# First squares, level sums and pooling sums from GpSimd to VectorE and ScalarE, and the pooling products one unit later

## The chip, the core and the metric

The kernel runs on one core of a Trainium2 chip. The metric is the device time of one execution in microseconds (us). Engines are named as the profile names them: PE (TensorE, matrix products), DVE (VectorE), ACT (ScalarE), POOL (GpSimd) and SP (SyncE, which here only issues DMAs). Each engine works through its own instructions in the order in which they were written.

## What is computed

Two layers of a decoder, for 256 tokens of a prompt and 8 sequences of 8 new tokens (320 tokens in all), with width 2048 and shared weights, in 32-bit floats:

```python
def trunk(...):
    for l in range(DEPTH):
        h = rmsnorm(x, norm_mix[l])
        m, s, b = mixer(h, ...)            # below
        x = x + m
        h = rmsnorm(x, norm_ffn[l])
        x = x + (jax.nn.silu(h @ w_gate[l]) * (h @ w_up[l])) @ w_down[l]
    return rmsnorm(x, norm_final), ...

def mixer(h, s_gla, buf, ...):
    proj = h @ w_in                        # q, k, v, g, gk_lr, u
    gk = jax.nn.log_sigmoid(gk_lr @ w_gk_up + b_gk) / GK_NORM
    o, s_new = gla(q, k, v, gk, s_gla)     # gated linear attention, causal
    o = rmsnorm(o, gla_norm) * jax.nn.silu(g)
    p, buf_new = pool_mixer(u, buf, ...)
    out = jnp.concatenate([o, p], axis=-1) @ w_out

def pool_mixer(u, buf, ...):               # windows 2, 4, 8, 16 for four groups of channels
    ext = jnp.concatenate([buf, u], axis=1)
    # per group: trailing mean over its window minus the token, then a 256x256 map
    y = einsum(mean - u, w_pool) * pool_scale
```

## The kernel before

Everything is kept transposed: features on the 128 partitions, the 320 tokens along a row. All weights pass through one stream of units. A unit is a block of up to 4 row tiles by 256 columns (512 KB); PE multiplies it into two output tiles of 128 x 320. To keep 32-bit accuracy each operand is split into a high and a low part, and every product is done three times (`mm3`, L145 to L147: high by high, high by low, low by high): 24 matmuls for a unit, 12 for a unit of a pooling map (two row tiles).

The loop `run` goes through the units. For unit i it loads up to unit i + 5 (four buffers `raw`, DMAs on SP), splits up to unit i + 2 (three buffers `hl`: ACT casts the high part at L109, DVE subtracts the low part at L110), reads out the accumulators that the unit before completed ("due" functions, `ev_...`), issues the unit's matmuls, and then lets every running generator do one step. The order in which the program text does this is the order of each engine's instructions; no scheduler moves anything. There are four accumulator tiles `acc`, two for a pair of output tiles.

The units of a layer's mixer stand in the order `IN_ORDER`: k and q, then u (the pooling inputs, four pairs 3, 2, 1, 0), then v and g. The pooling map of a group is a unit of its own (`pool_units`, "product 3" to "product 0" below), put among the four units of a later pair: product 3 among those of u1, product 2 among those of u0, and products 1 and 0 among those of v0.

Three pieces of work that the change touches run beside the stream:

- `first_squares` (L907 to L932 of before): the sum over features of x squared for the first norm, in tiles `qah` and `qal`, while the first weights and x arrive. `make_r` sums it over partitions with a matmul into `ps_r`, from which `r`, the norm's factor, is made.
- `level_gen`: the attention scores by eight levels of halving. Each level adds neighbouring sums in place: L430 on the half `Xv` (tile `PX`), L432 on the half `Pv` of the same tile, 640 elements a partition at levels 1, 2, 4 and 512 at the other five.
- `ev_u` and `pool_gen`: the outputs of a u pair are written into `EP` (prompt) and `ES` (samples) by DVE, the head of `ES` by a copy from `stg`, which SP loads. Trailing sums are then doubled, `AP` over `EP` (L578) and `AS` over `ES` (L579): one, two, three or four steps for windows 2, 4, 8, 16. L585 mends the first 16 positions, `so` takes the rows that go out by DMA (L592), and `d`, split into `dh` and `dl`, is the operand of the product. The product's outputs are read out by `split2` into `ph` (ACT, L122) and `pl` (DVE, L127).

Of the kernel before, what the change touches and what calls it, by code (L numbers as in the profile page):

```python
# [35 lines left out]
# columns of `vecs`, one 128-row column per feature tile  # L36
# [5 lines left out]
# pairs of 128-column tiles of w_in, in the order in which they are multiplied  # L42
# [12 lines left out]
class Unit:  # L55
    """A block of weights: nk row tiles by 256 columns, used by two output tiles."""
# [7 lines left out]
class Decoder:  # L64
# [40 lines left out]
    def split(self, hi, lo, src, scale=None):  # L105
        """hi + lo = src * scale, each of them with the 12 bits that the array multiplies."""
        nc = self.nc
        if scale is None:
            nc.scalar.copy(hi, src)  # L109
            nc.vector.tensor_tensor(lo, src, hi.bitcast(F32), ALU.subtract)  # L110
        else:
            nc.scalar.activation(hi, src, AF.Copy, scale=scale)  # L112
            nc.vector.scalar_tensor_tensor(lo, src, scale, hi.bitcast(F32), ALU.mult, ALU.subtract)  # L113

    def split2(self, his, los, srcs, scales=(None, None)):
        """Two splits, so that neither engine waits for the other's half."""
        nc = self.nc
        for hi, x, s in zip(his, srcs, scales):
            if s is None:
                nc.scalar.copy(hi, x)  # L120
            else:
                nc.scalar.activation(hi, x, AF.Copy, scale=s)  # L122
        for hi, lo, x, s in zip(his, los, srcs, scales):
            if s is None:
                nc.vector.tensor_tensor(lo, x, hi.bitcast(F32), ALU.subtract)
            else:
                nc.vector.scalar_tensor_tensor(lo, x, s, hi.bitcast(F32), ALU.mult, ALU.subtract)  # L127

    def rsqrt(self, out, src, scale):
        """out = 1 / sqrt(src * scale + EPS): exp(-log / 2), then a Newton step."""  # L130
        nc = self.nc
        h, t, y = (self.nrm.tile([P, T], F32, tag="rs_" + n, name="rs_" + n) for n in "hty")
        nc.scalar.activation(t, src, AF.Ln, scale=scale, bias=self.eps)
        nc.scalar.activation(y, t, AF.Exp, scale=-0.5)
        nc.vector.tensor_scalar(h, src, -0.5 * scale, -0.5 * EPS, ALU.mult, ALU.add)
        nc.vector.tensor_tensor(t, y, y, ALU.mult)
        nc.vector.tensor_tensor(t, t, h, ALU.mult)
        nc.vector.scalar_tensor_tensor(out, t, 1.5, y, ALU.add, ALU.mult)

# [9 lines left out]
    def pair_units(self, srcs, order, rhs, evac, nk=4):  # L149
        """Units that make one pair of output tiles: srcs[i] holds row tiles 4 i .. 4 i + 3."""  # L150
        box = {}
        units = []
        for n, i in enumerate(order):
            def mm(hl, n=n, i=i):
                if n == 0:
                    box["ps"] = [self.acc.tile([P, 512], F32, tag="acc", name="acc") for _ in range(2)]
                for j in range(2):
                    for k in range(nk):
                        xh, xl = rhs(i * nk + k)
                        self.mm3(box["ps"][j][:, :T], hl, k, j, xh, xl,  # L160
                                 n == 0 and k == 0, n == len(order) - 1 and k == nk - 1)
            ev = (lambda: evac([t[:, :T] for t in box["ps"]])) if n == len(order) - 1 else None
            units.append(Unit(srcs[i], nk, mm, ev))
        return units
# [52 lines left out]
    def add_square(self, m, x):  # L217
        """Adds x * x into the running sum over feature tiles."""
# [9 lines left out]
    def make_r(self):  # L228
        """After the last square: r = rsqrt(mean + eps) on every partition."""
        yield  # L230
        ps = self.smt("ps_r")
        self.nc.tensor.matmul(ps[:, :T], self.ones, self.sq_acc, start=True, stop=True)
        self.r = self.nrm.tile([P, T], F32, tag="r", name="r", bufs=2)
        yield
        self.rsqrt(self.r, ps[:, :T], 1.0 / D_MODEL)

    def new_x(self, ms, l, base):
        """Two tiles of x are final: the operands with the next norm's weight, and the squares."""
# [13 lines left out]
    def mixer_units(self, l):  # L252
# [7 lines left out]
        for n, (kind, i) in enumerate(IN_ORDER):  # L260
# [3 lines left out]
            if (kind, i) == ("v", 0):  # L264
                us[3:3] = self.pool_units(l, 0)
                us[2:2] = self.pool_units(l, 1)
            if (kind, i) == ("v", 1):
                us[0].start = self.open_late
            if kind == "u" and i < 2:
                us[2:2] = self.pool_units(l, i + 2)  # L270
# [4 lines left out]
        # w_out: the pooling half of the rows first  # L275
# [51 lines left out]
    def gk_gen(self, l):  # L327
        """log of the gates: P = 16 * gk = log_sigmoid(z), z = h w_gk w_gk_up + b."""
# [6 lines left out]
        # [hi | lo] of a row tile side by side: one pass multiplies both  # L335
# [31 lines left out]
    def level_gen(self):  # L367
        """Scores k_j . q_i exp(b_i - b_j) for j <= i, transposed. Tokens are halved again and
        again: at level s, a pair with i in the second and j in the first half of a group of 2 s
        takes exp(sum from the half's start to i) on q and exp(sum from j to the half's end) on k,  # L370
        so that no exponent is above zero."""
# [31 lines left out]
        for li, s in enumerate((1, 2, 4, 8, 16, 32, 64, 128)):  # L403
# [26 lines left out]
            nc.gpsimd.tensor_tensor(Xv[:, :, :, 0, :], Xv[:, :, :, 0, :],  # L430
# [3 lines left out]
            if s == 4:  # L434
                # whole sequences of the sample group
# [45 lines left out]
        # k decayed to the end of the prompt  # L481
# [23 lines left out]
    def put(self, p0, w, c0, src, copy=None):  # L505
        """Scores of both prompt tiles and all heads into rows p0.., columns c0.. of a tile."""
        # tile 0 starts at column 0 of a head's 384, tile 1 at 256
# [4 lines left out]
    def kd_sample(self):  # L512
        """k decayed to the end of its sequence, as 32 rows a sequence: hi, lo, hi, lo."""
# [22 lines left out]
    def stack(self, x, out, his, los):  # L536
        """x [P, n, 8, 8] into out [P, n, 8, 4, 8] as rows hi (at his) and lo (at los)."""
# [10 lines left out]
    # -- pooling  # L548
    def ev_u(self, ps, i):
# [12 lines left out]
        nc.gpsimd.tensor_copy(ES[:, :, :, 0:BUF], stg)  # L562
        self.gens.append(self.pool_gen(l, i, EP, ES))

    def pool_gen(self, l, i, EP, ES):
# [4 lines left out]
        # sums over trailing windows, doubling; only what the last one needs  # L570
# [3 lines left out]
        while s < w:  # L574
# [3 lines left out]
            nc.gpsimd.tensor_tensor(ap[:, :, lo:], cp[:, :, lo:], cp[:, :, lo - s : np_ - s], ALU.add)  # L578
            nc.gpsimd.tensor_tensor(as_[:, :, lo:], cs[:, :, lo:], cs[:, :, lo - s : ns_ - s], ALU.add)  # L579
# [4 lines left out]
        # the sequence's start: fewer positions than the window  # L584
        nc.gpsimd.tensor_tensor(cp[:, :, BUF : BUF + 16], cp[:, :, BUF : BUF + 16],  # L585
                                self.wcnt[:, i : i + 1, :].to_broadcast([P, 2, 16]), ALU.mult)
        # the buffers that go on: the last 15 rows
        so = early.tile([P, 2, NB + 1, BUF], F32, tag="so", name="so")
        nc.gpsimd.tensor_copy(so[:, :, 0:NB, :], ES[:, :, :, NS:])
        nc.gpsimd.tensor_copy(so[:, :, NB, :], EP[:, :, NP:])  # L590
# [32 lines left out]
    # -- values and gates, one head at a time  # L623
# [7 lines left out]
    def head_gen(self, h, vT):  # L631
# [33 lines left out]
        # rows of one sequence at a time, zero elsewhere  # L665
# [192 lines left out]
    def build(self):  # L858
# [4 lines left out]
        # x and the first weights arrive in turn  # L863
# [8 lines left out]
        # the array's clock rises once it has been busy for a while  # L872
# [34 lines left out]
    def first_squares(self):  # L907
        nc = self.nc
        q = [self.ffb.tile([P, 8, T], F32, tag=t, name="q" + t) for t in ("ah", "al")]
        for c in range(2):  # L910
            x = self.xT[:, 4 * c : 4 * c + 4, :]
            nc.gpsimd.tensor_tensor(q[0][:, 4 * c : 4 * c + 4, :], x, x, ALU.mult)
        add = lambda a, b: nc.gpsimd.tensor_tensor(a, a, b, ALU.add)
        add(q[0][:, 0:4], q[0][:, 4:8])
        for c in range(2):
            for _ in range(2):
                yield
            v = q[1][:, 4 * c : 4 * c + 4]
            nc.scalar.activation(v, self.xT[:, 8 + 4 * c : 12 + 4 * c, :], AF.Square)
            if c == 0:  # L920
                add(q[0][:, 0:4], v)
                v = q[0]
            add(v[:, 0:2], v[:, 2:4])
            add(v[:, 0], v[:, 1])
        self.sq_acc = self.nrm.tile([P, T], F32, tag="sqa", name="sqa")
        nc.gpsimd.tensor_tensor(self.sq_acc, q[0][:, 0], q[1][:, 4], ALU.add)
        nc.gpsimd.memset(self.sc, 0.0)
        nc.gpsimd.memset(self.scs, 0.0)
        while self.mf is None:
            yield  # L930
        nc.gpsimd.tensor_copy(self.masks, self.mf)
        yield from self.make_r()  # L932

    def _layer(self, l):
        units = self.mixer_units(l)
        st = self.st
        # the mixer's state is this layer's while its units run
# [10 lines left out]
    def finish(self, evacs):  # L948
        """The last tiles of x, and the last norm."""
# [25 lines left out]
def _pairs(w, cols):  # L975
    """[L, K, N] -> [L, N/256, K/512, 128, 4 * 256]: blocks in the order of use."""
# [7 lines left out]
def _cols(v):  # L984
    """[n * 128] -> [128, n]"""
# [74 lines left out]
```

## Time and profile before

| | |
|---|---|
| time, median of 3 runs | 2738.81 us (2738.59 to 2742.34) |
| span of the profiled execution, first to last instruction | 2735.4 us |
| PE busy | 2701.1 us, 99% of the span |
| DVE busy | 1351.9 us, 49% |
| ACT busy | 1067.3 us, 39% |
| POOL busy | 308.4 us, 11% |
| mean granted clock of TensorE | 0.985 of full speed |

The profile gives the profiled execution's span and no time of its own beside it; the runs were timed without a profile. Busy times of PE are modelled at their ends, as matmuls are pipelined. POOL's spans are rough.

### The profile page before, as it was taken

The numbers are of one execution on the slowest core, as the hardware profiler recorded it, in microseconds if no ns is written. First come the engines' busy times: TensorE is split into PE (matmuls) and PEld (weight loads), VectorE is DVE, ScalarE is ACT, GpSimd is POOL, SyncE is SP. The second block draws the span as 40 slices with busy tenths as digits, with TensorE's granted clock in tenths as the row PEclk, the third lists the DMA queues.
The fourth block names the chain that finished last, engine by engine and source line by source line (L and its number), as shares of the span: only waits on it lengthen the run. The fifth ranks groups of instructions, "written<-read, shape, count | busy, mean of one in ns | idle before, by whom it ended". The sixth has DMA issues, their size and how long they took to land.

```text
span 2735.4 us, 44895 instructions
## 1 busy us (share of the span) xinstructions
PE 2701.1 (99%) x19046; PEld 2680.6 (98%) x19046; DVE 1351.9 (49%) x1654; ACT 1067.3 (39%) x1344; POOL 308.4 (11%) x347
## 2 busy tenths in 40 slices
PE   8999999999999999999999999999999999999997
PEld 8999999999999999999999999999999999999997
DVE  6764455444444444444658544544444444444444
ACT  5444544333333333333444554443333333333334
POOL 3521111000000000000106211100000000000002
PEclk9999999999999999999999999999999999999998
DMA  5345544444444444444443544544444444444443
GB/s 189 117 155 166 161 151 147 153 148 150 151 148 153 147 152 148 149 152 147 148 140 108 184 162 142 154 147 148 153 147 152 149 151 150 149 153 147 152 149 108
DMA packets 115929, 408.67 MB, mean 149 GB/s; under 512 B 13264, under 2 KB 16848, under 8 KB 115728
## 3 DMA queue, kind: packets, MB, share of 16 engines
q1 hardware_dynamic: 115728, 405.80, 47.5%
q8 instruction: 149, 2.44, 0.4%
q14 instruction: 52, 0.43, 0.0%
HBM read 392.59 MB, written 13.16 MB: 148 GB/s over the span
## 4 chain that ended last, share of the span: by engine, by line
PE 95%; DVE 2%; issue 1%; POOL 1%; ACT 0%; DMA 0%; DVEq 0%; SPq 0%; ACTq 0%; POOLq 0%
PE acc L145 30%; PE acc L147 30%; PE acc L146 30%; PE ps_o L702 1%; DVE hl L110 1%; PE ps_o L704 0%; DVE xl L113 0%; PE ps_sn L683 0%; POOL PX L430 0%; POOL AS L579 0%; POOL AP L578 0%; PE ps_sp L719 0%; PE ps_o L700 0%; PE ps_o L705 0%; DVE xT L963 0%
## 5 line engine op out<-in xcount | busy, mean ns | idle before, releaser
L110 DVE TENSOR_TENSOR hl<-raw,hl 128x1024 fp32r<-128x1024 f32 (+1 forms) x729 | 921.7, 1265 | 1258.1 <-ACT hl L109 1257.3
L109 ACT CAST hl<-raw 128x1024 fp32r<-128x1024 f32 (+1 forms) x729 | 759.9, 1043 | 1312.7 <-PE acc L147 1232.9
L145 PE MATMUL acc<-xh,hl 128*128 128x320 f32 x3840 | 1195.7, 311 | 1.0 <-ACT xh L112 0.6
L147 PE MATMUL acc<-xh,hl 128*128 128x320 f32 x3840 | 1191.2, 310 | 2.7 <-DVE hl L110 2.7
L146 PE MATMUL acc<-xl,hl 128*128 128x320 f32 x3840 | 1191.5, 310 | 2.4 <-DVE xl L113 2.4
L145 PEld LDWEIGHTS acc<-xh,hl 128*128 128x128 f32 x3840 | 726.0, 189 | 4.3 <-ACT PX L359 0.9
L146 PEld LDWEIGHTS acc<-xl,hl 128*128 128x128 f32 x3840 | 725.5, 189 | 4.1 <-DVE xl L113 2.7
L147 PEld LDWEIGHTS acc<-xh,hl 128*128 128x128 f32 x3840 | 725.1, 189 | 3.8 <-DVE hl L110 3.7
L147 PE MATMUL acc<-ah,hl 128*128 128x320 f32 x1408 | 435.1, 309 | 0.0
L145 PE MATMUL acc<-ah,hl 128*128 128x320 f32 x1408 | 435.1, 309 | 0.0
L146 PE MATMUL acc<-al,hl 128*128 128x320 f32 x1408 | 435.1, 309 | 0.0
L145 PEld LDWEIGHTS acc<-ah,hl 128*128 128x128 f32 x1408 | 264.3, 188 | 0.0
L146 PEld LDWEIGHTS acc<-al,hl 128*128 128x128 f32 x1408 | 264.3, 188 | 0.0
L147 PEld LDWEIGHTS acc<-ah,hl 128*128 128x128 f32 x1408 | 264.3, 188 | 0.0
L783 POOL TENSOR_TENSOR ft<-ft,r 128x320 f32<-128x320 f32 x88 | 75.5, 880 | 1641.2 <-ACT ft L782 1629.4
L249 DVE TENSOR_TENSOR xT<-xT,acc 128x320 f32<-128x320 f32 x224 | 98.4, 481 | 5.8 <-PE acc L147 5.8
L226 POOL TENSOR_TENSOR sqa<-sqa,sq 128x320 f32<-128x320 f32 x58 | 51.0, 880 | 309.1 <-ACT sq L225 307.0
L145 PE MATMUL acc<-ph,hl 128*128 128x320 f32 x256 | 79.1, 309 | 0.0
L146 PE MATMUL acc<-pl,hl 128*128 128x320 f32 x256 | 79.1, 309 | 0.0
L147 PE MATMUL acc<-ph,hl 128*128 128x320 f32 x256 | 79.1, 309 | 0.0
L145 PE MATMUL acc<-oh,hl 128*128 128x320 f32 x256 | 79.1, 309 | 0.0
L146 PE MATMUL acc<-ol,hl 128*128 128x320 f32 x256 | 79.1, 309 | 0.0
(197 smaller groups left out, 1604.9 us busy)
## 6 DMA issues: line engine op xcount, KB each, us to landing
raw<-in_w_gu SPq DMA_DIRECT2D x352, 512.0 KB, 3.6
raw<-in_w_down SPq DMA_DIRECT2D x176, 512.0 KB, 3.6
raw<-in_w_in SPq DMA_DIRECT2D x127, 512.0 KB, 3.8
raw<-in_w_out SPq DMA_DIRECT2D x64, 512.0 KB, 3.7
S<-in_s SPq DMA_DIRECT2D x16, 512.0 KB, 4.8
out_s_sample<-S SPq DMA_DIRECT2D x16, 512.0 KB, 2.9
raw<-in_w_pool SPq DMA_DIRECT2D x8, 256.0 KB, 2.8
xT<-in_xT SPq DMA_DIRECT2D x3, 640.0 KB, 7.2
```

The source lines that it names most:

```text
L109: nc.scalar.copy(hi, src)
L110: nc.vector.tensor_tensor(lo, src, hi.bitcast(F32), ALU.subtract)
L145: nc.tensor.matmul(ps, wh, xh, start=first, stop=False)
L146: nc.tensor.matmul(ps, wh, xl, start=False, stop=False)
L147: nc.tensor.matmul(ps, wl, xh, start=False, stop=last)
L226: nc.gpsimd.tensor_tensor(self.sq_acc, self.sq_acc, s, ALU.add)
L249: self.nc.vector.tensor_tensor(self.xT[:, m, :], self.xT[:, m, :], p, ALU.add)
L702: nc.tensor.matmul(po[:, NP + 8 * b : NP + 8 * b + 8], S[b // 4][:, b % 4, vc], st["q8"][:, h, 8 * b : 8 * b + 8], start=False, stop=(b == ...
L783: self.nc.gpsimd.tensor_tensor(t, t, self.r, ALU.mult)
```

## The change

The first squares go from two POOL multiplications and two ACT squares to four ACT squares; their sums, the sums at L430 of all levels, the doubling sums and L585 go from POOL to DVE; the copies of `stg` into `ES`, those into `so` and the cast of the masks go from POOL to ACT. The memsets of `sc` and `scs` stay on POOL but come early. The pooling products 3, 2 and 1 stand one unit later in their pair's units. Product 0's line is unchanged. Numbers of lines below are those of each file. The diff's core (comments that were dropped are left out):

```diff
             if (kind, i) == ("v", 0):
                 us[3:3] = self.pool_units(l, 0)
-                us[2:2] = self.pool_units(l, 1)
+                us[3:3] = self.pool_units(l, 1)
...
             if kind == "u" and i < 2:
-                us[2:2] = self.pool_units(l, i + 2)
+                us[3:3] = self.pool_units(l, i + 2)
...
-            nc.gpsimd.tensor_tensor(Xv[:, :, :, 0, :], Xv[:, :, :, 0, :],
+            nc.vector.tensor_tensor(Xv[:, :, :, 0, :], Xv[:, :, :, 0, :],
                                     Pv[:, :, :, 1, s - 1 : s].to_broadcast(shape), ALU.add)
...
-        nc.gpsimd.tensor_copy(ES[:, :, :, 0:BUF], stg)
+        nc.scalar.copy(ES[:, :, :, 0:BUF], stg)
...
-            nc.gpsimd.tensor_tensor(ap[:, :, lo:], cp[:, :, lo:], cp[:, :, lo - s : np_ - s], ALU.add)
-            nc.gpsimd.tensor_tensor(as_[:, :, lo:], cs[:, :, lo:], cs[:, :, lo - s : ns_ - s], ALU.add)
+            nc.vector.tensor_tensor(ap[:, :, lo:], cp[:, :, lo:], cp[:, :, lo - s : np_ - s], ALU.add)
+            nc.vector.tensor_tensor(as_[:, :, lo:], cs[:, :, lo:], cs[:, :, lo - s : ns_ - s], ALU.add)
...
-        nc.gpsimd.tensor_tensor(cp[:, :, BUF : BUF + 16], cp[:, :, BUF : BUF + 16],
+        nc.vector.tensor_tensor(cp[:, :, BUF : BUF + 16], cp[:, :, BUF : BUF + 16],
...
-        nc.gpsimd.tensor_copy(so[:, :, 0:NB, :], ES[:, :, :, NS:])
-        nc.gpsimd.tensor_copy(so[:, :, NB, :], EP[:, :, NP:])
+        nc.scalar.copy(so[:, :, 0:NB, :], ES[:, :, :, NS:])
+        nc.scalar.copy(so[:, :, NB, :], EP[:, :, NP:])
...
     def first_squares(self):
         nc = self.nc
         q = [self.ffb.tile([P, 8, T], F32, tag=t, name="q" + t) for t in ("ah", "al")]
-        for c in range(2):
-            x = self.xT[:, 4 * c : 4 * c + 4, :]
-            nc.gpsimd.tensor_tensor(q[0][:, 4 * c : 4 * c + 4, :], x, x, ALU.mult)
-        add = lambda a, b: nc.gpsimd.tensor_tensor(a, a, b, ALU.add)
-        add(q[0][:, 0:4], q[0][:, 4:8])
-        for c in range(2):
-            for _ in range(2):
-                yield
-            v = q[1][:, 4 * c : 4 * c + 4]
-            nc.scalar.activation(v, self.xT[:, 8 + 4 * c : 12 + 4 * c, :], AF.Square)
+        add = lambda a, b: nc.vector.tensor_tensor(a, a, b, ALU.add)
+        acc = q[0][:, 0:4]
+        for c in range(4):
+            v = q[c // 2][:, 4 * (c % 2) : 4 * (c % 2) + 4]
+            nc.scalar.activation(v, self.xT[:, 4 * c : 4 * c + 4, :], AF.Square)
             if c == 0:
-                add(q[0][:, 0:4], v)
-                v = q[0]
-            add(v[:, 0:2], v[:, 2:4])
-            add(v[:, 0], v[:, 1])
+                nc.gpsimd.memset(self.sc, 0.0)
+                nc.gpsimd.memset(self.scs, 0.0)
+            else:
+                add(acc, v)
+            for _ in range((1, 1, 2, 0)[c]):
+                yield
+        add(acc[:, 0:2], acc[:, 2:4])
         self.sq_acc = self.nrm.tile([P, T], F32, tag="sqa", name="sqa")
-        nc.gpsimd.tensor_tensor(self.sq_acc, q[0][:, 0], q[1][:, 4], ALU.add)
-        nc.gpsimd.memset(self.sc, 0.0)
-        nc.gpsimd.memset(self.scs, 0.0)
+        nc.vector.tensor_tensor(self.sq_acc, acc[:, 0], acc[:, 1], ALU.add)
         while self.mf is None:
             yield
-        nc.gpsimd.tensor_copy(self.masks, self.mf)
+        nc.scalar.copy(self.masks, self.mf)
```

Three places show what this does to the order of an engine's instructions. A name's number tells tiles of one name apart; `x2` is the same instruction twice.

DVE at the program's start, behind the first two blocks of weights: before, the splits of the weights (`hl`) and of x (`xl`) follow each other.

```order
L113 SCALAR_TENSOR_TENSOR xl<-xT,vecs,xh 128x320 x4
L110 TENSOR_TENSOR hl<-raw,hl 128x1024 x2
L113 SCALAR_TENSOR_TENSOR xl<-xT,vecs,xh 128x320 x4
L110 TENSOR_TENSOR hl<-raw,hl 128x1024 x2
L113 SCALAR_TENSOR_TENSOR xl<-xT,vecs,xh 128x320 x4
L110 TENSOR_TENSOR hl<-raw,hl 128x1024 x3
```

Of the change, the same place of DVE, with the sums of squares (`qah`, `qal`, `sqa`) among them:

```order
L113 SCALAR_TENSOR_TENSOR xl<-xT,vecs,xh 128x320 x4
L110 TENSOR_TENSOR hl<-raw,hl 128x1024 x2
L910 TENSOR_TENSOR qah<-qah 128x1280
L113 SCALAR_TENSOR_TENSOR xl<-xT,vecs,xh 128x320 x4
L110 TENSOR_TENSOR hl<-raw,hl 128x1024
L910 TENSOR_TENSOR qah<-qah,qal 128x1280
L110 TENSOR_TENSOR hl<-raw,hl 128x1024
L113 SCALAR_TENSOR_TENSOR xl<-xT,vecs,xh 128x320 x4
L110 TENSOR_TENSOR hl<-raw,hl 128x1024
L910 TENSOR_TENSOR qah<-qah,qal 128x1280
L910 TENSOR_TENSOR qah<-qah 128x640
L924 TENSOR_TENSOR sqa<-qah 128x320
```

Five sums now stand between the splits, the last two ahead of the splits of the seventh and eighth following block.

DVE at the end of layer 0's pooling stage, before: `dl` belongs to the operand of product 0, the two groups of `pl` (L127) read out product 1 and product 0, and each `hl` of 1024 is the split of one unit of weights.

```order
L110 TENSOR_TENSOR dl<-d,dh 128x640
L110 TENSOR_TENSOR hl<-raw,hl 128x1024
L127 SCALAR_TENSOR_TENSOR pl<-acc,vecs,ph 128x320 x2
L110 TENSOR_TENSOR hl<-raw,hl 128x1024 x2
L127 SCALAR_TENSOR_TENSOR pl<-acc,vecs,ph 128x320 x2
```

DVE at the same place, of the change:

```order
L110 TENSOR_TENSOR dl<-d,dh 128x640
L110 TENSOR_TENSOR hl<-raw,hl 128x1024 x2
L127 SCALAR_TENSOR_TENSOR pl<-acc,vecs,ph 128x320 x2
L110 TENSOR_TENSOR hl<-raw,hl 128x1024
L127 SCALAR_TENSOR_TENSOR pl<-acc,vecs,ph 128x320 x2
```

Two splits now precede the reading out of product 1, and one lies between the two readings.

PE at the end of layer 0's pooling stage, of the change: `dh_1700` is the operand of product 1, `dh_1880` that of product 0, `hl_1799` and `hl_1829` their weights, `acc_...` the accumulators.

```order
L145 MATMUL acc_1890<-dh_1700,hl_1799 128x320
L146 MATMUL acc_1890<-dl_1701,hl_1799 128x320
L147 MATMUL acc_1890<-dh_1700,hl_1799 128x320
L145 MATMUL acc_1914<-dh_1880,hl_1829 128x320
L146 MATMUL acc_1914<-dl_1881,hl_1829 128x320
L147 MATMUL acc_1914<-dh_1880,hl_1829 128x320
```

Before, 24 matmuls of a unit of v0 stood between the two products, ahead of product 0 with these rows (`xh` is the operand of v0, `dh_1872` that of product 0):

```order
L145 MATMUL acc_1765<-xh_82,hl_1801 128x320
L146 MATMUL acc_1765<-xl_83,hl_1801 128x320
L147 MATMUL acc_1765<-xh_82,hl_1801 128x320
L145 MATMUL acc_1916<-dh_1872,hl_1831 128x320
L146 MATMUL acc_1916<-dl_1873,hl_1831 128x320
```

That unit has moved ahead of product 1, and products 1 and 0 follow each other.

## Rows read from the trace of the kernel before

**Rows 1.** The page: engine, busy us, share of the span, instructions.

```profile
PE 2701.1 (99%) x19046; PEld 2680.6 (98%) x19046; DVE 1351.9 (49%) x1654; ACT 1067.3 (39%) x1344; POOL 308.4 (11%) x347
```

**Rows 2.** Waits of PE, whole span: us in total, times, longest us.

```profile
PE acc L145 <- DVE ES L560: 6.4, 2, 3.4
PE acc L145 <- DVE pl L127: 3.0, 2, 1.7
PE acc L147 <- DVE hl L110: 2.7, 3, 1.5
PE acc L146 <- DVE xl L113: 2.4, 1, 2.4
...
PE ps_kq L529 <- DVE Ds L451: 0.8, 1, 0.8
PE acc L145 <- ACT xh L112: 0.6, 1, 0.6
```

**Rows 3.** Timeline, DVE at the start: start us, us, instructions, idle time before.

```profile
6.33 3.13 DVE L113 SCALAR_TENSOR_TENSOR xl<-xT,vecs,xh 128x320 fp32r<-128x320 f32 x2
...
9.99 1.00 DVE L113 SCALAR_TENSOR_TENSOR xl<-xT,vecs,xh 128x320 fp32r<-128x320 f32 x2
...
12.05 6.71 DVE L113 SCALAR_TENSOR_TENSOR xl<-xT,vecs,xh 128x320 fp32r<-128x320 f32 x4
...
20.95 6.58 DVE L113 SCALAR_TENSOR_TENSOR xl<-xT,vecs,xh 128x320 fp32r<-128x320 f32 x4
```

**Rows 4.** Timeline, POOL at the start.

```profile
6.33 2.32 POOL L912 TENSOR_TENSOR qah<-xT 128x1280 f32<-128x1280 f32 x1 [5.50 <-DMA xT<-in_xT]
```

**Rows 5.** Timeline, ACT at the start.

```profile
7.89 0.62 ACT L109 CAST hl<-raw 128x512 fp32r<-128x512 f32 x1 [1.29 <-DMA raw<-in_w_in]
...
19.71 1.27 ACT L919 ACTIVATE qal<-xT 128x1280 f32<-128x1280 f32 x1
```

**Rows 6.** Windows: stretch, its us, busy us by engine, granted clock, DMA share, GB/s.

```profile
7.80:14.60 6.80, 5.55 (x21) 5.55 (x22) 6.80 (x8) 5.33 (x9) 4.58 (x3) 0.50 1.02 411
97.00:172.00 75.00, 69.78 (x758) 67.69 (x757) 63.30 (x88) 35.41 (x55) 51.04 (x58) 0.95 0.39 119
124.00:130.60 6.60, 5.76 (x24) 5.35 (x24) 6.60 (x7) 4.30 (x6) 6.60 (x6) 0.50 0.31 97
350.00:400.00 50.00, 50.00 (x343) 50.00 (x342) 26.64 (x31) 21.22 (x30) 7.04 (x8) 1.00 0.49 148
1472.20:1478.90 6.70, 5.52 (x22) 5.36 (x23) 6.24 (x11) 3.35 (x5) 6.70 (x8) 0.50 0.32 104
1515.00:1525.00 10.00, 8.30 (x59) 8.03 (x58) 6.01 (x10) 5.96 (x10) 6.69 (x15) 1.00 0.64 189
```

The engines in these rows stand in the order PE, weight loads of PE, DVE, ACT, POOL.

**Rows 7.** Groups by shape, DVE, 95 to 172 us: busy us, mean ns | idle before.

```profile
L110 DVE TENSOR_TENSOR hl<-raw,hl 128x1024 fp32r<-128x1024 f32 x15 | 22.3, 1484 | 1.1 <-ACT hl L109 0.8
L432 DVE TENSOR_TENSOR PX<-PX 128x512 f32<-128x512 f32 x5 | 6.0, 1190 | 3.2 <-POOL PX L430 3.2
...
L432 DVE TENSOR_TENSOR PX<-PX 128x640 f32<-128x640 f32 x2 | 3.4, 1689 | 1.8 <-POOL PX L430 1.8
L110 DVE TENSOR_TENSOR dl<-d,dh 128x640 fp32r<-128x640 f32 x4 | 3.4, 838 | 3.2 <-ACT dh L109 3.2
```

**Rows 8.** Timeline, DVE in a stretch in which POOL rests.

```profile
143.04 0.69 DVE L422 TENSOR_TENSOR Q<-Q,qk 128x512 f32<-128x512 f32 x1
143.64 0.69 DVE L427 TENSOR_TENSOR K<-K,qk 128x512 f32<-128x512 f32 x1
```

**Rows 9.** Timeline, ACT and DVE around product 1's reading out, layer 0.

```profile
167.53 1.05 ACT L109 CAST hl<-raw 128x1024 fp32r<-128x1024 f32 x1
...
168.61 1.22 DVE L110 TENSOR_TENSOR hl<-raw,hl 128x1024 fp32r<-128x1024 f32 x1
...
169.76 1.00 DVE L127 SCALAR_TENSOR_TENSOR pl<-acc,vecs,ph 128x320 fp32r<-128x320 f32 x2
```

**Rows 10.** Timeline, POOL, third pooling group of layer 0.

```profile
144.94 0.78 POOL L562 COPY ES<-stg 128x240 f32<-128x240 f32 x1 [7.13 <-DMA stg<-in_bufT]
```

More of the change, by code (lines that the diff above doesn't have):

```diff
@@ L909, in first_squares @@
         q = [self.ffb.tile([P, 8, T], F32, tag=t, name="q" + t) for t in ("ah", "al")]
-        for c in range(2):
-            x = self.xT[:, 4 * c : 4 * c + 4, :]
-            nc.gpsimd.tensor_tensor(q[0][:, 4 * c : 4 * c + 4, :], x, x, ALU.mult)
-        add = lambda a, b: nc.gpsimd.tensor_tensor(a, a, b, ALU.add)
-        add(q[0][:, 0:4], q[0][:, 4:8])
-        for c in range(2):
-            for _ in range(2):
-                yield
-            v = q[1][:, 4 * c : 4 * c + 4]
-            nc.scalar.activation(v, self.xT[:, 8 + 4 * c : 12 + 4 * c, :], AF.Square)
-            if c == 0:
-                add(q[0][:, 0:4], v)
-                v = q[0]
-            add(v[:, 0:2], v[:, 2:4])
-            add(v[:, 0], v[:, 1])
+        add = lambda a, b: nc.vector.tensor_tensor(a, a, b, ALU.add)
[3 more added lines that the diff above has]
+            nc.scalar.activation(v, self.xT[:, 4 * c : 4 * c + 4, :], AF.Square)
+            if c == 0:
+                nc.gpsimd.memset(self.sc, 0.0)
[3 more added lines that the diff above has]
+            for _ in range((1, 1, 2, 0)[c]):
+                yield
+        add(acc[:, 0:2], acc[:, 2:4])
         self.sq_acc = self.nrm.tile([P, T], F32, tag="sqa", name="sqa")
-        nc.gpsimd.tensor_tensor(self.sq_acc, q[0][:, 0], q[1][:, 4], ALU.add)
-        nc.gpsimd.memset(self.sc, 0.0)
-        nc.gpsimd.memset(self.scs, 0.0)
+        nc.vector.tensor_tensor(self.sq_acc, acc[:, 0], acc[:, 1], ALU.add)
         while self.mf is None:
             yield
-        nc.gpsimd.tensor_copy(self.masks, self.mf)
+        nc.scalar.copy(self.masks, self.mf)
         yield from self.make_r()
```

## The prediction

> **What bounds the kernel now.** I read the page first: TensorE (PE) is busy for 2701.1 of 2735.4 us [rows 1]. So nothing that frees another engine is worth anything by itself; only what shortens the 34 us in which PE is not busy, or what raises its clock, shows in the time. The waits of PE then say where those 34 us lie [rows 2]: apart from the lead-in and the last norm, which the edit leaves alone, PE waits in the first 45 us (2.4 for `xl`, and 0.9 and 1.5 of the 2.7 for `hl`) and in the pooling stage of each layer (6.4 for `ES` in two waits, 3.0 for `pl` in two, 0.8 at `ps_kq`, 0.3 of `hl`). All but a fraction end on VectorE (DVE). [...]
>
> Why DVE is late is seen where GpSimd (POOL) works beside it. Two splits `xl` take 3.13 us while POOL squares for 2.32 us, and 1.00 us a little later with POOL idle [rows 3, 4]; four take 6.71 instead of 2.0. In the pooling stage the sum L432 of 512 elements takes 1190 ns in the mean [rows 7], where one of that size takes 690 ns alone [rows 8].
>
> **The start.** Removed from POOL: two squares, the adds, the cast of the masks; ScalarE (ACT) gets four squares of 1.27 us each (its present square, [rows 5]) and the masks, DVE three adds of 1280 elements (1.5 us each at 1.17 ns an element, below), one of 640 and one of 320: 5.6 us. DVE gets back far more: 2.1 us on the first pair, 4.7 and 4.6 on the two groups of four behind it [rows 3]. Step by step: the first `xl` pair ends at 6.33 + 1.00 = 7.3 instead of 9.46 us. PE then does the first six matmuls and must wait for the second half of the first block, whose cast on ACT begins at 7.89 because its load lands then [rows 5]; that stays. Cast to 8.5, DVE's split to 9.2, the next `xl` pair to 10.2 (now 11.0). Behind it PE has 14 matmuls of that block left, 0.146 us each at full clock, 0.264 at half (50.00 over 343 and 5.55 over 21, [rows 6]): it ends at 12.2 or at 13.9, where now 23 matmuls at half clock from 9.05 end at 15.1. That is 3.0 us earlier, or 1.2 if the clock falls all the same. Behind that the two waits for `hl` of 0.9 and 1.5 us [rows 2], whose splits stand behind the slow `xl` groups in DVE's order, go: 2.4 us. ACT's squares stand between its casts, which by the same adding up end some 3 to 5 us before PE comes to their blocks: they cost nothing, and with that cover gone 1.27 each. PE asks for the sum of squares after six blocks, at 12.2 + 5 x 3.6 = 30.2; DVE has by then, from 10.2 on, six splits of 1.15, twelve `xl` of 0.49 and the sums, 18.4 us, and perhaps 1.5 of waits for ACT: 30.1. This is the tightest place, and I put nothing on it. Sum: 5.4 us, or 3.6 at half clock. I take 5.4: the two waits that now lie together (0.6 and 2.4) become 0.6, 0.2, 1.0 and 0.4, all under the 1.7 that left the clock at full [rows 6].
>
> **The pooling stage: DVE's account.** Added to DVE per layer: eight level sums (4480 elements), ten sums over `AP` (5212), ten over `AS` (2016), four small products. Two instructions of 512 follow each other in 0.60 us [rows 8], 1.17 ns an element with overhead: 13.9 us, and as the short ones carry more overhead an estimated 14.5. Taken off it by POOL's silence: fifteen splits of 1484 ns that take 1.22 alone [rows 7, 9], 4.0; five L432 of 512, 2.5; two of 640 at 1689 ns, against 0.82 by the same rate, 1.7; that is 8.2 in three groups, and with the smaller ones I take 11. DVE was busy 63.3 of 75 us [rows 6], so 66.8 follows: still under 75, with its waits for POOL gone. The moved copies (240 and 30 elements) go to ACT, busy 35.4 of 75. So on average it fits; but it comes unevenly, since levels, pooling difference and its split meet in single units, and DVE's cover is the look-ahead of two units, 7 us. I allow 1.5 us of new short PE waits a layer for that (0 to 3.4).
>
> **A new wait on ACT.** `ES` is completed by a copy that waits for the load `stg`. POOL now sits 7.13 us for it [rows 10]; on ACT it is queued before the next cast of weights, and DVE's sum of `ES` before the next split. SP issues it earlier after the change, since `out_pool_out` ahead of it waits for copies that ACT does at once. I cost it at nothing, covered by the look-ahead of 7 us; at worst the 7.13 less that cover, nothing to speak of, at each of two places a layer.
>
> **The products one unit later.** Product 3 waits until DVE has read the accumulators of the group before. One more unit (3.5 us of PE) ahead of it is longer than the 3.0 and 3.4 it waited, and the relief comes on top: this wait, the one at `ps_kq` and the half clock behind them go. Gone in layer 0: 3.0 + 0.8 + 1.3, and half of the 5.76 us of PE at half clock, 2.9: 8.0. In layer 1: 3.4 + 0.3 + 1.7 + 2.8 = 8.2 [rows 2, 6].
>
> But product 1 now stands right in front of product 0. There are four accumulators, and the values' pair is open, so product 0 takes product 1's pair, and nothing lies between. When product 1 ends, ACT first casts the next weights (they wait for the buffer that product 1 frees), DVE splits them behind that, then `pl` is written: 1.05 + 1.15 + 0.5, with the hops between them 2.8 us [rows 9], against 1.3 and 1.7 now, when a whole unit lay between. Bounds: 1.3 if ACT and DVE were through at once, 3.4 if DVE is late as well. And 2.8 lies nearer to the waits after which the clock fell (2.4 with 0.6, 3.0, 3.4) than to 1.7; I take it that it falls: half of 6.8, 3.4 us. New per layer: 2.8 + 3.4 + 1.5 = 7.7; net gain 0.3 and 0.5 us.
>
> **Sum.** 5.4 + 0.3 + 0.5 = 6.2 us. The profiled span of 2735.4 lies 3.4 us under the median of the runs, 2738.8, which I take as what lies around it: 2729.2 in the span, **2732.6 us** in a run.
>
> **Rivals.** (a) The start falls to half clock as now: gain 4.4, 2734.4. (b) The clock holds at one new wait (2729.2, or 2731.0 with a), or at both (2725.8): for it speaks that dense work stands on both sides of a single wait shorter than 3.0; against it the 2.4 at the start.
>
> (c) The work only changes its engine: what POOL no longer slows down is spent again by the added sums, and the start gains nothing; 2738.8 - 0.8 = 2738.0. In the pooling stage the account (14.5 against 11) looks like that; at the start it does not (5.6 against 11.4). [...]
>
> (d) Slower: DVE becomes the bound of the pooling stage. If the strided sums on DVE cost 1.9 times my price, as contended ones do now (1190 against 690, 1689 against 820), they take 27.6 us; 63.3 - 11 + 27.6 with 3.2 of its own waits for `dh` [rows 7] is 83.1 of the 75 us there are, +8.1 a layer, 2738.8 - 5.4 + 16.2 = 2749.6. It decides from 19.5 us of moved work, 1.34 times my estimate. [...]
>
> **How the numbers follow.** A difference of 0.2% (5.5 us) is about what a measurement of this kernel can tell. Both new waits with the clock falling 0.50 (start at full clock 0.30, case a 0.20); b with one 0.25, with both 0.10; c 0.07; d 0.08. Faster by over 0.2% is under 2733.3: some six tenths of the first, a third of a, nearly all of b, 0.58; slower 0.07; the rest, 0.35, within. The range leaves out most of d and the far end of b: 2726 to 2738.5; the likeliest case alone spans 2730.5 to 2735, by the 0 to 3.4 of the short waits.
>
> **What would show it.** `xl` pairs of 1.0 us and no `hl` wait of PE before 36 us; the eighth block done 4 to 5 us earlier; no PE wait of over 1 us in front of product 3; a PE wait of 2.5 to 3 us ended by `pl` between products 1 and 0 in both layers, with a clock of 0.50 behind it; DVE 65 to 69 us busy in the 75 us. I am wrong if PE waits for `hl` in several units of the stage (d), if ACT is seen held by `stg`, or if `ps_r` waits for the sum of squares.

## The result, and the profile after

The changed kernel takes 2753.7 us (median of 4 runs, 2752.79 to 2755.27) beside 2738.7 us before (4 runs, 2738.29 to 2742.34): 1.0056 of it, with a 95% interval of 1.0044 to 1.0068. It is 15 us slower; 6 us faster was forecast.

The page after, engines: busy us, share of the span, instructions.

```profile
PE 2708.2 (98%) x19046; PEld 2686.2 (98%) x19046; DVE 1347.0 (49%) x1723; ACT 1076.4 (39%) x1371; POOL 193.7 (7%) x249
```

POOL lost 115 us of work and DVE, which took most of it, is not busier than in [rows 1]. PE is busy 7 us longer with the same instructions, and its mean granted clock is 0.982 where it was 0.985. The span is 18.1 us longer than the profiled one of before; what is left of that should be waits. The waits of PE after, whole span (total us, times, longest):

```profile
PE acc L145 <- DVE pl L127: 23.6, 6, 5.6
PE acc L145 <- ACT xh L112: 1.6, 2, 0.9
PE ps_warm L875 <- DVE ones L870: 1.1, 1, 1.1
PE acc L147 <- DVE hl L110: 1.0, 4, 0.3
PE acc L146 <- DVE xl L113: 0.6, 2, 0.3
```

Beside [rows 2], the 6.4 us for `ES`, the 2.4 for `xl` and most of those for `hl` and at `ps_kq` are gone. One line grew from 3.0 to 23.6 us: six waits for `pl`, the reading out of pooling products. The timeline of PE says where (the three of layer 0; layer 1 has the same three):

```profile
131.63 0.63 PE L145 MATMUL acc<-xh,hl 128*128 128x320 f32 x1 [5.63 <-DVE pl L127]
...
154.25 0.41 PE L145 MATMUL acc<-xh,hl 128*128 128x320 f32 x1 [0.77 <-DVE pl L127]
...
173.11 0.63 PE L145 MATMUL acc<-dh,hl 128*128 128x320 f32 x1 [5.40 <-DVE pl L127]
```

The third multiplies `dh` and is product 0, where a wait was forecast. The first two multiply `xh`: they are the first matmul of u0 and the first of v0, which read nothing of a pooling product. The windows of after (PE, weight loads, DVE, ACT, POOL, granted clock, DMA share, GB/s):

```profile
5.00:36.00 31.00, 28.79 (x191) 27.69 (x190) 25.32 (x35) 26.39 (x36) 0.00 (x0) 1.00 0.83 293
97.00:172.00 75.00, 63.67 (x709) 61.03 (x708) 58.50 (x106) 35.25 (x63) 5.50 (x15) 0.95 0.38 112
130.95:137.78 6.83, 6.15 (x23) 6.15 (x24) 6.32 (x14) 2.13 (x4) 0.00 (x0) 0.50 0.57 174
171.91:178.74 6.83, 5.63 (x21) 5.63 (x22) 2.51 (x4) 2.17 (x4) 0.00 (x0) 0.50 0.47 150
```

The start now runs at full clock; behind each of the two long waits PE works at 0.50, in both layers (in layer 1 from 1492.87 to 1499.70 and from 1533.83 to 1540.66 us); its matmuls start every 0.267 us there and every 0.147 at 1.00. Set side by side by the first matmul of named tiles, the changed kernel is 5.6 us ahead at `ps_r` and at `ps_z` of layer 0, 5.3 behind at layer 0's first `ps_vt` (after the pooling stage), 6.7 behind when layer 1 begins, 16.5 behind at layer 1's first `ps_vt`, 18.1 at the end. So the start gives 5.6 and the two pooling stages take 10.8 and 9.7. The 3 us left are lost among the attention heads behind each pooling stage: both kernels have stretches at half clock there, 23.9 us of them a layer before and 27.3 after. Half of the 3.4 us more, an estimate from the clock of 0.50, is 1.7 us a layer; why they grew was not tried.

What stands in front of the first wait is seen on DVE, and in the rows below that on ACT (timelines of after):

```profile
127.13 0.69 DVE L596 SCALAR_TENSOR_TENSOR d<-AP,EP 128x512 f32<-128x512 f32 x1
127.74 0.36 DVE L598 SCALAR_TENSOR_TENSOR d<-AS,ES 128x64 f32<-128x64 f32 x2
128.94 0.83 DVE L110 TENSOR_TENSOR dl<-d,dh 128x640 fp32r<-128x640 f32 x1 [0.84 <-ACT dh L109]
129.89 1.23 DVE L110 TENSOR_TENSOR hl<-raw,hl 128x1024 fp32r<-128x1024 f32 x1
131.03 1.00 DVE L127 SCALAR_TENSOR_TENSOR pl<-acc,vecs,ph 128x320 fp32r<-128x320 f32 x2
```

```profile
128.19 0.72 ACT L109 CAST dh<-d 128x640 fp32r<-128x640 f32 x1 [2.26 <-DVE d L598]
128.82 1.04 ACT L109 CAST hl<-raw 128x1024 fp32r<-128x1024 f32 x1
129.76 0.94 ACT L122 ACTIVATE ph<-acc,vecs 128x320 fp32r<-128x320 f32 x2
```

Product 3 ended on PE at 121.1 us; it is read out 10 us later, behind the difference `d` of group 2, its `dh` and `dl`, and a split of weights. In front of the third wait it is ACT:

```profile
167.75 0.72 ACT L109 CAST dh<-d 128x640 fp32r<-128x640 f32 x1 [5.53 <-PE acc L147]
168.38 1.04 ACT L109 CAST hl<-raw 128x1024 fp32r<-128x1024 f32 x1
169.33 1.06 ACT L502 COPY kdt<-ps_kd 128x512 f32<-128x512 f32 x2
170.28 1.05 ACT L109 CAST hl<-raw 128x1024 fp32r<-128x1024 f32 x1
171.23 0.96 ACT L122 ACTIVATE ph<-acc,vecs 128x320 fp32r<-128x320 f32 x2
```

There is one buffer `dh`. ACT sits 5.53 us until product 1, its reader, has ended; then it casts `dh` and does four more casts and copies before it reads product 1 out.

So the theory (P in the expectations below) was: the new **places** cost the time, through the accumulators (product 3's are wanted by u0) and the one `dh`. The rival (D) was the prediction's (d): DVE has more work than it can do.

### The profile page after: what moved, and what is told of

Read it like the earlier page. It is cut to its first block, busy times and chain, and to the rows that moved or that the text cites. A ratio compares the mean times of both kernels' runs of the same rounds, so it can differ in the third digit from the quotient of the medians.

```text
span 2753.5 us, 44867 instructions
## 1 busy us (share of the span) xinstructions
PE 2708.2 (98%) x19046; PEld 2686.2 (98%) x19046; DVE 1347.0 (49%) x1723; ACT 1076.4 (39%) x1371; POOL 193.7 (7%) x249
## 5 line engine op out<-in xcount | busy, mean ns | idle before, releaser
L110 DVE TENSOR_TENSOR hl<-raw,hl 128x1024 fp32r<-128x1024 f32 (+1 forms) x729 | 910.9, 1250 | 1280.3 <-ACT hl L109 1279.5
L145 PE MATMUL acc<-xh,hl 128*128 128x320 f32 x3840 | 1197.4, 312 | 14.8 <-DVE pl L127 12.8
L145 PE MATMUL acc<-oh,hl 128*128 128x320 f32 x256 | 79.1, 309 | 0.0
L147 PE MATMUL acc<-oh,hl 128*128 128x320 f32 x256 | 79.1, 309 | 0.0
```

The costliest lines, as they stand in the source:

```text
L145: nc.tensor.matmul(ps, wh, xh, start=first, stop=False)
L147: nc.tensor.matmul(ps, wl, xh, start=False, stop=last)
```

## The experiments

Each time is the median; the kernel before ran beside each group on the same chip, at 2738.2 to 2739.1 us. Ratios are to it.

**Engines or places.** The first run is the changed kernel with the products at their old places, the second the kernel before with the products at the new ones; the third is the changed kernel with product 1 alone put back (the upper pair of lines below), the fourth with products 3 and 2 (the lower pair); the first has both pairs, and the second has them the other way round on the kernel before.

```diff
-                us[3:3] = self.pool_units(l, 1)
+                us[2:2] = self.pool_units(l, 1)
...
-                us[3:3] = self.pool_units(l, i + 2)
+                us[2:2] = self.pool_units(l, i + 2)
```

> The work is on its new engines, the pooling products stand where they stood before the change. Theory P (the places of the products cost the time: product 3 so close in front of u0 that its accumulators are not read out in time, product 1 right in front of product 0 with one buffer dh): both waits of 5.6 and 5.4 us go to under 2 us each, the half clock behind them goes, the gain of 5.5 us at the start stays; about 2727 us (2723 to 2732), faster than before. Rival D (VectorE has more work in the pooling stage than it can do): the waits only move to other units, the stage still loses about 10 us a layer; 2748 to 2756.

> The three pooling products stand one unit later, all work stays on the engines of before. Theory P: slower than before, with a wait for pl in front of u0's first unit and one in front of product 0, each with half clock behind it: about 2752 us (2745 to 2762). Rival D: the places alone cost nothing much or gain a little, as the wait in front of product 3 goes: 2733 to 2741.

> The changed kernel with product 1 alone back at its old place, one unit ahead of product 0. Theory P: the wait of 5.4 us in front of product 0 falls to about 1.5 and the 3.4 us that its half clock costs go, the 5.64 in front of u0 stays: about 7 us less a layer, 2740 us (2736 to 2744). Rival D: a wait of the same size shows at another unit behind it, 2750 to 2756.

> The changed kernel with products 3 and 2 back at their old places, product 1 stays right in front of product 0. Theory P: the waits of 5.64 and 0.77 us in front of u0 and v0 and the half clock behind the first go (9 to 10 us a layer), against which product 3 may wait up to 2 us again; the 5.4 stays: about 2739 us (2734 to 2744). Rival D: the wait comes back in front of product 3 at its full size, 2748 to 2756.

Measured: engines alone 2732.2 us (0.9976, 0.9966 to 0.9985), places alone 2765.5 (1.0096, 1.0083 to 1.0110), product 1 back 2737.7 (0.9995, 0.9986 to 1.0004), products 3 and 2 back 2743.1 (1.0015, 1.0006 to 1.0023). Theory P gave 2727, 2752, 2740 and 2739. The directions are its own, but the first two times lie outside the ranges it had stated (the first by 0.2 us, the second by 3.5): it put the places' price too low (26.8 us on the old engines) and the gain of the engines too high. The rival's 2748 to 2756 came in none of the first, third and fourth, and in the second not its 2733 to 2741. Waits of PE in the engines-only run:

```profile
PE ps_kq L529 <- DVE Ds L451: 3.2, 2, 1.6
...
PE ps L469 <- DVE K L427: 1.6, 2, 0.9
PE acc L145 <- DVE ES L560: 1.6, 2, 0.8
...
PE acc L145 <- DVE pl L127: 1.5, 1, 1.5
```

DVE is a little late in the stage (this is what is true of rival D), but no wait is over 1.6 us and the whole stage of layer 0 runs at full clock (layer 1 has one stretch of 3.4 us at 0.50, from about 1509.7 us):

```profile
97.00:172.00 75.00, 69.01 (x751) 66.12 (x742) 63.13 (x112) 37.84 (x67) 7.00 (x15) 1.00 0.43 136
```

In the places-only run one line says it:

```profile
PE acc L145 <- DVE pl L127: 22.4, 4, 6.2
```

With products 3 and 2 back the two waits of 5.40 stay and those in front of u0 are gone; with product 1 back it is the other way round (two of 5.64, two of 0.8). First the run with products 3 and 2 back, then that with product 1 back:

```profile
PE acc L145 <- DVE pl L127: 10.8, 2, 5.4
```

```profile
PE acc L145 <- DVE pl L127: 12.8, 4, 5.6
```

So each place makes its own wait, and the waits add up: 10.8 and 12.8 are the 23.6 us of the changed kernel. The times do not quite: product 1 back makes the changed kernel 16.0 us faster, products 3 and 2 back 10.6, all three together 21.5; where the difference lies was not traced. With products 3 and 2 at their old places, shorter waits for DVE's other work come back (3.2 us for `Ds` and 1.6 for `ES`, with product 1 at either place).

**What u0 waits for.** Three edits of the changed kernel, one at a time. In the first, ACT copies product 3's accumulators to SBUF, and `ph` and `pl` are made from the copy:

```diff
         def evac(ps):
...
+            if i == 3:
+                ts = [self.nrm.tile([P, T], F32, tag="sq", name="sq", bufs=2) for _ in range(2)]
+                for t, p in zip(ts, ps):
+                    self.nc.scalar.copy(t, p)
+                ps = ts
```

> The changed kernel, but ScalarE first copies product 3's two accumulators to SBUF, and ph and pl are made from the copy; VectorE's order stays. In the changed kernel ScalarE comes to ph at 129.76 us, VectorE to pl at 131.03. Theory A (u0's first unit waits for product 3's accumulators and for nothing else): the wait ends with ScalarE's copy of the first accumulator, about 130.3 instead of 131.6, and is put down to ScalarE: 4.3 to 4.7 us instead of 5.64; 2751 us (2748 to 2753). Rival (what is waited for is VectorE's result or its place in the queue): still 5.6 us, ended by VectorE; 2754 or more.

Measured 2750.9 us (1.0046, 1.0031 to 1.0061), and the first matmul of u0 (timeline of PE) and the copy (of ACT) read:

```profile
131.70 0.63 PE L145 MATMUL acc<-xh,hl 128*128 128x320 f32 x1 [4.24 <-ACT sq L621]
```

```profile
131.23 0.74 ACT L621 COPY sq<-acc 128x320 f32<-128x320 f32 x2
```

The wait ends with ACT's first copy, while `pl` comes only at 132.50: u0 waits for the accumulators to be read and not for what is made from them. The next two change the order in the queues. One puts a product's readout ahead of the next cast and split (in `run`, ahead of the loads and splits; `pool` marks a product's unit), the other makes the difference of group 2 a unit later (in `pool_gen`):

```diff
+            if i and us[i - 1].pool:
+                due, self.later = self.later, []
+                for f in due:
+                    f()
...
-        if w <= 4:
+        if w <= 8:
             yield
```

> The changed kernel with only this edit: a product's ph and pl stand ahead of the next cast and split of weights. Theory Q (the order of the queues): the wait in front of u0 falls by a cast or split, about 1.2 us, to 4.4; that in front of product 0 by the 1.2 to 1.9 us of cast and split, to 3.5 to 4.2; 2748 us (2744 to 2751). Rival (other work is late in their place): 2752 to 2755.

> The changed kernel with only this edit: the difference d of group 2 (L596, L598, dh, dl) is made one unit later, so that it stands behind the readout of product 3. In the changed kernel these take VectorE from 127.13 to 129.77 us and hold ScalarE 2.26 us at dh. Theory Q: the wait in front of u0 falls by 2 to 2.6 us, to 3.0 to 3.6; the 5.40 in front of product 0 stays; 2749 us (2744 to 2751). Rival: the wait moves to another unit of u0 or to product 2, 2752 to 2755.

Measured: readout first 2745.3 us (1.0022, 1.0012 to 1.0031), wait in front of u0 4.29, in front of product 0 3.75, the one of 0.77 gone. Difference later 2747.4 (1.0032, 1.0019 to 1.0045), 2.88 in front of u0, 5.40 kept. The first matmul of u0, first with the readout first, then with the difference later:

```profile
131.67 0.41 PE L146 MATMUL acc<-xh,hl 128*128 128x320 f32 x1 [4.29 <-DVE pl L128]
```

```profile
128.48 0.41 PE L145 MATMUL acc<-xh,hl 128*128 128x320 f32 x1 [2.88 <-DVE pl L127]
```

The waits came where theory Q put them or a little lower: of the 5.6 us, 1.35 go with the cast and split ahead of the readout and 2.75 with `d`, `dh` and `dl`.

**What product 0 waits for.** Product 0 gets a `dh` and `dl` of its own (in a buffer `K` that is idle then):

```diff
+        if i == 0:
+            two = early.tile([P, H * T], F32R, tag="K", name="dh0", bufs=2).rearrange("p (a c t) -> p a c t", a=2, c=2)
+            dh, dl = two[:, 0], two[:, 1]
...
```

> The changed kernel, but product 0's dh and dl lie in a buffer of their own, so that ScalarE's cast of dh need not wait for product 1's end. Theory (the single buffer dh is what made the wait in front of product 0 5.4 instead of the 2.8 us of the prediction): the wait falls to 2.8 to 3.3 us, 2.3 us a layer: 2749 us if the clock still falls behind it, 2742 if it holds. Rival (ScalarE and VectorE are late for other reasons, the buffer is only what the trace names): still over 5 us, 2752 to 2755. The 5.64 in front of u0 stays in either case.

Measured 2749.7 us (1.0040, 1.0026 to 1.0053). PE's wait in layer 0 (layer 1 has the same 2.90), and three windows, columns as above: the first behind the wait in front of product 0, the other two behind that in front of u0, which stays (5.64 in layer 0, 5.63 in layer 1):

```profile
170.72 0.64 PE L145 MATMUL acc<-dh,hl 128*128 128x320 f32 x1 [2.90 <-DVE pl L127]
```

```profile
170.22:173.63 3.41, 2.91 (x11) 2.91 (x12) 0.90 (x2) 0.00 (x0) 0.00 (x0) 0.50 0.52 162
132.67:136.08 3.41, 2.86 (x11) 2.86 (x12) 3.38 (x7) 0.55 (x1) 0.00 (x0) 0.50 0.60 182
1487.77:1494.60 6.83, 5.26 (x20) 5.26 (x21) 6.61 (x13) 3.02 (x6) 0.00 (x0) 0.50 0.47 141
```

2.90 against the prediction's 2.8: cast, split, `pl`, once the buffer is out of the way. The clock falls behind it as forecast, but for 3.41 us and not 6.8, so that by estimate, at a clock of 0.50, it costs half of the 2.91 us of PE in it (3.41 in layer 1), not 3.4.

**Both mended.** The last three edits together (own `dh`, readout first, difference later) on the changed kernel; the same on the old engines; and the first of these with the copies into `ES` and `so` back on POOL.

> The changed kernel with the products at their new places, and their readouts brought forward in the queues of ScalarE and VectorE: product 0 has its own dh and dl, a product's ph and pl stand ahead of the next cast and split of weights, and the difference d of group 2 comes one unit later. Theory (it is not the place as such but what stands in the two queues ahead of the readout): the wait in front of u0 falls from 5.64 to about 2.5 us, that in front of product 0 from 5.4 to about 1.5, with full clock behind both: 2725 us, or 2732 if the clock still falls behind the first. Rival (the place itself costs it, since VectorE is 6 us or more behind at product 3's end whatever its order): the first wait stays over 4.5 us and the time over 2738.

> All work on the engines of before, the products at their new places, with the readouts brought forward in the queues as above. Theory Q (what the new places cost is the order of the two queues, whoever does the sums): the waits of 6.2 and more us in front of u0 and product 0 shrink to under 2.5 us, and the time falls from 2765 to 2732 to 2740. Rival (with GpSimd beside it VectorE cannot be in time at the new places, the moves of engines are needed for it): the first wait stays over 4 us, 2745 to 2756.

> The changed kernel with the readouts of the products brought forward in the queues (as in the run before), and the copies of stg into ES and so back on GpSimd. The copies gave 1 us or nothing at the old places; here the two waits left in the stage are for pl (1.75 and 0.5 to 1.0 us), which stands behind VectorE's own work and not behind the copies: 2727 to 2729, no difference that can be told from 2728.4. Rival (ScalarE's wait for stg sets the rest): 2725 to 2726.

Measured 2728.4 us (0.9961, 0.9949 to 0.9974), 2740.6 (1.0011, 1.0002 to 1.0020) and 2726.7 (0.9960, 0.9946 to 0.9973). The first and the third can't be told apart; either beats both kernels. The second lies 0.6 us above theory Q's range; its waits in front of u0 and product 0 are 1.40 and 0.70 us in layer 0 and 0.58 and 0.54 in layer 1, under the 2.5 that Q gave. In the mended kernel on the new engines the wait in front of product 0 is 0.49 and 1.02 us, and u0 still waits, but for 1.75 us:

```profile
129.65 0.41 PE L146 MATMUL acc<-xh,hl 128*128 128x320 f32 x1 [1.75 <-DVE pl L128]
```

and in that with the copies back 97 to 172 us runs at full clock, with DVE busy for 65.0 of them:

```profile
97.00:172.00 75.00, 70.20 (x772) 67.56 (x763) 65.00 (x116) 36.36 (x58) 12.04 (x25) 1.00 0.44 134
```

The six times (us) in one table:

| | old places | new places | new places, queues mended |
|---|---|---|---|
| old engines | 2738.7 | 2765.5 | 2740.6 |
| new engines | 2732.2 | 2753.7 | 2728.4 |

The places cost 21 to 27 us as written, and 2 us or less than nothing (-4) when the queues are mended; the engines gain 6.5, 11.8 and 12.2.

**What each move is worth, at the old places.** First the kernel before with the new first squares alone; then the engines-only kernel with one thing put back on POOL at a time: the copies into `ES` and `so`, the level sums (L430), the pooling sums (L578, L579, L585). Each edit is the change's own lines, taken or undone.

> The kernel before with the new first squares alone (and the masks' cast on ScalarE). The prediction's term for the start was 5.4 us: 2733.3 us (2732 to 2734.5), no half clock in the first 36 us, all marks behind it earlier by that. Rival (the work only changes its engine): 2737.5 to 2739. Together with the run that has all moves of engines at the old places (2732.2) it also says what the moves in the pooling stage are worth: about 0.5 us a layer if this one comes to 2733.3.

> All moves of engines at the old places, except that the copies of stg into ES and into so go back to GpSimd. In the run with the copies on ScalarE the copy waits 2.95 us for its load in front of product 0, and the casts behind it are late. Theory (that wait on ScalarE is worth something after all, against the prediction that costed it at nothing): the gaps of 0.69 and 1.47 us in front of and at product 0 shrink by 0.5 to 1.5 us a layer, 2729.5 to 2731. Rival (it is hidden, as costed): 2732, the same.

> All moves of engines at the old places, but the level sums (L430) back on GpSimd. Theory (in the pooling stage a sum that goes to VectorE costs about what GpSimd's silence gives back, so that neither move alone matters much): 2731 to 2734, no difference from the run with all moves at the old places that can be told. Rival (the level sums on VectorE are what makes it late there, waits for Ds and K): 1 to 2 us less a layer, 2728 to 2730. Other rival (GpSimd beside VectorE is what costs): 2735 to 2738.

> All moves of engines at the old places, but the pooling sums over AP and AS and L585 back on GpSimd. Theory as for the level sums: 2731 to 2735. Rival (without the ten to twenty pooling sums VectorE is in time, the waits at ps_kq and for K go): 2728 to 2730. Other rival (GpSimd beside VectorE is what costs): wait in front of product 3 of 3 us again and half clock behind it, 2736 to 2739.

Measured: squares alone 2734.3 us (0.9984, 0.9975 to 0.9993); copies back 2731.3 (0.9973, 0.9962 to 0.9985); level sums back 2733.0 (0.9980, 0.9971 to 0.9989); pooling sums back 2738.4 (1.0001, 0.9992 to 1.0010). Beside the 2732.2 of all moves, the copies and the level sums make no difference that can be told. Nor do all moves of the stage together, 2 us beyond the squares alone. The exception goes against what theory expected: with the pooling sums alone on POOL and the level sums on DVE the kernel is 6 us slower than with both on DVE. The second rival of that run, POOL beside DVE, gave this time (2736 to 2739) and nearly this wait: the largest is for the readout of u2 in front of product 3, 2.5 us in each layer (the line below) with half clock behind it (the mean clock is 0.98 over 97 to 172 and over 1455 to 1530 us), where all moves leave 0.8. But POOL beside DVE is not the whole cause. With the level sums on POOL instead the time is 2733.0, and with both on POOL it is 2734.3 (at the edge of the intervals), though the wait for `ES` is up to 3.2 us there. What else makes this mixture slow was not found.

```profile
PE acc L145 <- DVE ES L560: 5.0, 2, 2.5
```

## Why the prediction was wrong

By the prediction's own terms, in us (layer 0 / layer 1):

| term | forecast | measured |
|---|---|---|
| start | -5.4 | -5.6 |
| waits and half clock of before that go | -8.0 / -8.2 | gone, as listed |
| product 0's wait | 2.8 | 5.40 / 5.40 |
| half clock behind it | 3.4 | 2.8 / 2.6 (half of the 5.63 and 5.12 us of PE at 0.50) |
| new short waits | 1.5 | 1.4 (0.77, 0.27, 0.23, 0.14) |
| wait in front of u0 | none | 5.63 / 5.64 |
| half clock behind that | none | 3.1 / 2.6 (half of 6.15, of 5.21) |

The last column gives 18.3 and 17.6 a layer of new waits; less the 8.0 and 8.2 that go, +10.3 and +9.4, where the marks in the traces say 10.8 and 9.7. The halves are estimates from the granted clock. The forecast's 3.4 is half of 6.8 us, the length of the first stretch at 0.50 in [rows 6]; behind product 0's wait that clock lasted 6.83 us in both layers, but PE was not busy in all of it.

**The step that failed** is "The products one unit later". It asked what product 3 waits for, and that was right: no wait stands in front of product 3 any more. It did not ask who waits for product 3. The same sentence on the four accumulators that was used for product 0 ("takes product 1's pair") holds for u0: its first unit takes product 3's pair, and moving product 3 one unit later took one of the two units away in which that pair was read out. This is 8.7 of the 10.6 us by which layer 0 misses the forecast, and 8.2 of the 9.9 of layer 1. That u0 waits for these accumulators is shown by the copy on ACT (4.24 us, ended by ACT), that the place makes the wait by the run with products 3 and 2 back.

**The mis-sized term** is product 0's wait, 5.4 instead of 2.8. Its parts were right (2.90 with a `dh` of its own); left out was that the step moves `dh` as well. With a unit between the two products the single buffer came free in time; without it ACT's queue stood still behind that cast. This is 2.6 us a layer, of which 0.6 and 0.8 are offset by a half clock that cost less than forecast: the other 2 us.

**Right**: the start, with `xl` pairs of 1.01 us. That it came to within 0.2 us of 5.4 is luck of this profile, as the last section shows; in time the squares alone gave 4.1, with an interval of 1.9 to 6.8 around it (0.0007 to 0.0025 of 2738). Right too: the `stg` copy on ACT, costed at nothing. The prediction named an ACT held by `stg` as a sign of being wrong, and ACT was held (3.51 us for the third group of layer 0 in the changed kernel, 4.59 in the engines-only one); but undoing the copies changes the time by only 0.9 and 1.7 us, within the intervals. The short waits had the right size partly by luck: of the 1.4 us, 0.77 is in front of v0, for product 2's readout, which is the failed step again at a smaller size; it goes when products 3 and 2 go back. DVE's account, 65 to 69 of 75 us, can't be read from the changed kernel, where DVE was held up itself (58.5). In the two mended kernels on the new engines it is 64.9 and 65.0 in layer 0, where 63.3 was before, but 59.3 in layer 1 (1455 to 1530 us), where 62.0 was before: at best the lower end.

**The rivals.** (d) ended on the right side and near the right time (2749.6) for the wrong reason: with the same sums on DVE the time is 2726.7 to 2732.2. (c), that work only changes its engine, fits the pooling stage at the old places (2 us for all its moves), not the start. At the new places the moves gain 12 us; a likely reason, not tested, is that DVE's lateness is waited for at more points there. (b) was about smaller things than what happened. (a), the start at half clock, did not happen in this profile, but in others with the same start.

## What to carry to other kernels

When a unit is moved in a stream, ask for every buffer that it holds (accumulators, operands) who takes it next, and how far away that is now; the wait that was removed in front of the unit may stand behind it, larger. Read from the order of each queue what precedes the readout: here two edits of order and one buffer were worth 25 us at the same places. An edit of two halves is worth measuring in halves: these were -6.5 and +26.8 us (together +15, as they don't simply add).

## What was not expected of the hardware

The same wait does not always cost the same clock. Behind the wait of 5.64 us in front of u0 the clock was at 0.50 for 6.83 us in the changed kernel in both layers, and in the run with its own `dh` for 3.41 us in layer 0 and 6.83 in layer 1. Behind the 1.75 us of the mended kernel it fell in layer 0 and not in layer 1 (1.74 there):

```profile
130.64:134.05 3.41, 3.41 (x15) 3.41 (x14) 2.71 (x6) 0.63 (x1) 0.12 (x1) 0.50 0.54 160
1477.63:1481.04 3.41, 3.40 (x23) 3.41 (x24) 3.38 (x6) 0.00 (x0) 0.00 (x0) 1.00 0.55 147
```

In the mended kernel on the old engines even a wait of 2.70 us, in front of v0 in layer 0, left it at 1.00 (PE's wait, then the window behind it):

```profile
157.80 0.41 PE L146 MATMUL acc<-xh,hl 128*128 128x320 f32 x1 [2.70 <-DVE pl L128]
```

```profile
157.80:161.20 3.40, 3.40 (x23) 3.40 (x24) 2.98 (x4) 3.40 (x6) 0.00 (x0) 1.00 0.20 39
```

The prediction took 1.7 us as safe (the wait for `pl` near 1520 us of before) and 2.4 as not (that for `xl` near 9 us); the traces here don't give such a line, and what decides it was not tried.

The start varies in the same way. Of the fourteen profiles with the new first squares, eight came to `ps_r` 5.5 to 6.4 us earlier than the one of before; the other six came only 3.7 to 4.2 us earlier, and in these PE had a stretch at 0.50 near 10 us, as in the prediction's case (a) (the mean clock over 5 to 36 us is 0.94 in the mended kernel on the new engines, one of the six, and 1.00 in the changed kernel, one of the eight). A gain read from one profile's start can thus be off by some 2 us.
